# Decay exponential, rotated copies and six orderings in a two-layer hybrid decoder kernel

## The chip, the cores and the metric

The kernel runs on one core of a Trainium2 chip. The metric is the device time of one execution in microseconds. A comparison of two kernels takes timed runs of both on the same chip; beside them, one execution of each is profiled, and that one has a time of its own. All engine times in this document are from such a profile, counted from the start of its span.

The engines: TensorE (PE, with its weight loads as PEld), VectorE (DVE), ScalarE (ACT), GpSimd (POOL) and SyncE (SP), which issues the transfers. Each works through its own instructions strictly in the order they were laid down. They meet through semaphores.

## The reference, cut to what matters

Two layers over 512 tokens of width 1024, all in float32:

```python
def hybrid_layer(x, cos, sin, ...):
    xn = rmsnorm(x, norm1_g)
    proj = xn @ w_in          # split into SSD, MLA, GatedDeltaNet parts and three gate logits
    y_ssd = ssd_mixer(...)    # chunked scan; output normed in two groups of 512 channels
    y_mla = mla_mixer(mla_cq, mla_ckv, mla_kr, cos, sin, ...)
    y_gdn = gdn_mixer(...)
    mixed = g_ssd * (y_ssd @ w_ssd_out) + g_mla * (y_mla @ w_mla_out) + g_gdn * (y_gdn @ w_gdn_out)
    h = x + mixed @ w_out
    f = jnp.square(jax.nn.relu(rmsnorm(h, norm2_g) @ w_up)) @ w_down
    return h + f

def mla_mixer(cq, ckv, k_rope, cos, sin, q_norm_g, w_uq, kv_norm_g, w_ukv):
    q = (rmsnorm(cq, q_norm_g) @ w_uq)       # 8 heads of 128 plain + 64 rotated
    kv = (rmsnorm(ckv, kv_norm_g) @ w_ukv)   # 8 heads of 128 keys and 128 values
    k_pe = apply_rope(k_rope, cos, sin)      # one rotated key for all heads
    # scores = q_nope . k_nope + q_pe . k_pe, causal softmax, times v

a = -jnp.exp(a_log)                          # decay rates of SSD (and likewise of GatedDeltaNet)
```

A final RMS norm follows the second layer.

## The kernel before

**Precision.** A float32 product is made of three products of a faster kind: each operand is split into a high part (a rounding cast on ACT) and a low part (the difference, on DVE), and `mm3` (L196) issues high by high, high by low, low by high. So every weight tile and every activation needs one ACT and one DVE operation before PE can use it: `split_half` (L165; its rows are whi L170 and wlo L171) for weights, `split_act` (L268) and `split_gain` (L273, rows L274 and L275, with a gain per channel) for activations.

**Layout and staging.** Activations stand transposed, channels on partitions: `xh`, `xl` are eight tiles of 128 channels by 512 tokens. `norm_half` (L299) makes them for one half of the tokens: two token tiles are scaled by their inverse root mean square (xr, in the feed-forward f, L306), then turned by 16 transposes on PE (L311), four to a PSUM bank, each bank followed by two `split_gain`. The banks come from `sm_bank`, a rotating set of three; `y_bank` (tiles named yt) is a single bank beside them, `acc_bank` a set of four that products accumulate in. `norm_half` runs eight times: both halves of the first norm and of the second norm, in two layers.

**One layer.** The first products are those of the front: the key latent (256 wide, ck), the rotary key (64 wide, kr) and the step sizes, 352 columns in all (`front_weights`, L333, and `front`, L399). Then come the query latent (cq, L536), the transposes of the normed key latent (`latent`, L522), the rope tables in layer 0 (`rope_tables`, L119, sine and cosine on ACT) and attention in four pairs of heads (hp 0 to 3). `rope` (L545) swaps halves by four transfers on SP, multiplies by cosine (L551) and by sine (L552), adds. The rotated key kpe goes into kz0 and kz1, its rounded copy in one half of the partitions and zeros in the other, and into kps, the rounded copy below and the rest above. The rotated query of a pair of heads is cast to qph, and four transfers (L633) spread its halves over the tiles qps. The scores of a head and a query tile are five products: three of the plain part (L674 to L676), one of qps with kps (L677), one of qpl with kz (L678). The probabilities are turned on PE (L695) and multiplied with the values (L712 to L714).

The SSD and GatedDeltaNet branches follow, each SSD group normed by sums of squares that a product with ones makes (L832, one per chunk t of 128 tokens); between their steps PE runs output products of other branches (`out_proj`, L493). The output projection and the down projection use seven instead of eight block products (`seven`, L1204), for which DVE forms sums of weight blocks (`plus` in `seven_weights`, L1183, its row L1189). `up` (L1392) runs the up projection in four quarters qd of four blocks of 256 columns c each, through `dense_F` (L204).

`step_sizes` (L427) computes the decays, with aexp = exp(a_log) at L450, once per layer. ACT holds one set of function tables at a time: sine needs another set than exponential and tanh.

**What sets the order.** A planner puts each engine's instructions in order from what they depend on and from estimated costs. Code inside `tc.high_priority()` is placed as early as it can be. `behind(key, instruction)` (L153) makes the planner lay an instruction behind the one that `place(key, ...)` (L160) marks; `dense_F` and `dense_T` mark each weight tile of a tagged product by (tag, k, j). It is an order without a wait. So an edit at one place can move rows elsewhere.

## Time and profile before

| | |
|---|---|
| median of 3 runs | 2260.42 us (2259.19 to 2260.94) |
| the profiled execution's own time | 2263.41 us |
| its span, first to last instruction | 2261.6 us |
| mean granted clock of TensorE | 0.998 |
| PE, DVE, ACT, POOL busy | 2246.2, 1638.1, 1167.3, 65.7 us |
| read from HBM | 225.53 MB |

A row of a timeline gives the start, the duration, the engine, the line of the kernel, the operation, output and inputs, shapes, how many instructions it stands for, and in brackets the idle time of the engine before it and what ended it. [...] A row of windows gives the stretch, its length, then busy time and number of instructions of PE, PEld, DVE, ACT and POOL, the granted clock of PE, the share of the transfer engines and GB/s. A row of waits names who waited for whom: total, times, longest.

### The profile page before, as it was taken

Reading aid. Unit: us, or ns where it says so; the run is one execution under the profiler, and the core shown is the slowest. Engines: PE = TensorE matmul, PEld = TensorE weight load, DVE = VectorE, ACT = ScalarE, POOL = GpSimd, SP = SyncE. Lnnn points to the kernel's source line nnn. Section 1 sums busy time; section 2 is a strip of 40 time slices with the busy share of each in tenths; the row PEclk is TensorE's granted clock in tenths of the full one; section 3 lists DMA queues with packets and bytes.
Section 4 is the critical chain, followed back from the end, with each engine's and each line's share of the span. In section 5 each row is a group of like instructions: output and inputs, shape, how many; then the busy total and the mean of one; then the engine's idle time right before and its main releaser. Section 6 shows DMA issues by size and latency. Waiting matters only on the chain.

```text
span 2261.6 us, 32000 instructions
## 1 busy us (share of the span) xinstructions
PE 2246.2 (99%) x11758; PEld 1867.3 (83%) x11758; DVE 1638.1 (72%) x3259; ACT 1167.3 (52%) x2378; POOL 65.7 (3%) x84
## 2 busy tenths in 40 slices
PE   9999999999999999999999999999999999999998
PEld 8888787888888888888888888888888888888887
DVE  7777567876667778767877775678758668778668
ACT  6556644333443555554656566443335445645546
POOL 1000000000000000000010000000001000000000
PEclk9999999999999999999999999999999999999999
DMA  4333633452225143233133336335422251432231
GB/s 144 91 94 94 195 103 121 132 147 73 80 75 177 57 149 112 86 102 121 48 105 91 90 111 197 98 118 149 122 79 80 66 185 39 168 112 100 87 112 47
DMA packets 221310, 246.16 MB, mean 109 GB/s; under 512 B 34513, under 2 KB 172641, under 8 KB 221153
## 3 DMA queue, kind: packets, MB, share of 16 engines
q1 hardware_dynamic: 221008, 243.86, 35.3%
q8 instruction: 92, 1.51, 0.3%
q14 instruction: 66, 0.53, 0.1%
q10 hardware_dynamic: 144, 0.26, 0.0%
HBM read 225.53 MB, written 11.74 MB: 105 GB/s over the span
## 4 chain that ended last, share of the span: by engine, by line
PE 93%; DVE 3%; ACT 1%; DMA 1%; issue 1%; POOL 0%; SPq 0%; POOLq 0%; ACTq 0%; DVEq 0%
PE acc L198 24%; PE acc L202 23%; PE acc L201 23%; PE sm L202 3%; PE sm L198 3%; PE sm L201 3%; DVE wlo L171 1%; PE sm L695 1%; PE sm L1082 1%; PE sm L800 1%; PE yt L202 1%; PE yt L198 1%; PE yt L201 1%; PE sm L1108 1%; DVE ckl L737 1%
## 5 line engine op out<-in xcount | busy, mean ns | idle before, releaser
L171 DVE TENSOR_TENSOR wlo<-wraw,whi 128x512 fp32r<-128x512 f32 (+1 forms) x536 | 365.0, 686 | 328.8 <-ACT whi L170 321.7
L170 ACT CAST whi<-wraw 128x512 fp32r<-128x512 f32 (+1 forms) x536 | 329.5, 617 | 514.6 <-PE acc L201 347.1
L198 PE MATMUL acc<-xh,whi 128*128 128x512 f32 (+1 forms) x1344 | 525.5, 392 | 0.0
L202 PE MATMUL acc<-xh,wlo 128*128 128x512 f32 (+1 forms) x1344 | 520.5, 388 | 0.8 <-DVE wlo L171 0.8
L201 PE MATMUL acc<-xl,whi 128*128 128x512 f32 (+1 forms) x1344 | 519.1, 387 | 0.0
L202 PEld LDWEIGHTS acc<-xh,wlo 128*128 128x128 f32 x1344 | 252.6, 188 | 51.2 <-DVE wlo L171 1.8
L201 PEld LDWEIGHTS acc<-xl,whi 128*128 128x128 f32 x1344 | 252.9, 188 | 48.2 <-DVE xl L275 0.7
L198 PEld LDWEIGHTS acc<-xh,whi 128*128 128x128 f32 x1344 | 252.7, 188 | 48.2 <-ACT xh L274 0.4
L170 ACT CAST whi<-wr 128x512 fp32r<-128x512 f32 x168 | 104.4, 621 | 109.5 <-PE acc L201 47.2
L198 PE MATMUL acc<-yh,whi 128*128 128x512 f32 x384 | 152.4, 400 | 0.0
L201 PE MATMUL acc<-yl,whi 128*128 128x512 f32 x384 | 150.7, 392 | 0.0
L202 PE MATMUL acc<-yh,wlo 128*128 128x512 f32 x384 | 150.4, 392 | 0.0
L171 DVE TENSOR_TENSOR wlo<-wr,whi 128x512 fp32r<-128x512 f32 x168 | 113.1, 687 | 35.4 <-ACT whi L170 34.4
L737 DVE SCALAR_TENSOR_TENSOR ckl<-acc,pc,ckl 128x511 f32<-128x511 f32 (+2 forms) x168 | 120.8, 743 | 19.5 <-ACT ckl L733 10.3
L198 PEld LDWEIGHTS acc<-yh,whi 128*128 128x128 f32 x384 | 71.6, 188 | 16.1 <-ACT yh L274 2.2
L202 PEld LDWEIGHTS acc<-yh,wlo 128*128 128x128 f32 x384 | 72.2, 188 | 14.6
L201 PEld LDWEIGHTS acc<-yl,whi 128*128 128x128 f32 x384 | 72.2, 188 | 14.1
L198 PE MATMUL acc<-whi,xh 128*128 128x512 f32 (+1 forms) x208 | 80.0, 385 | 0.3 <-DVE ckl L737 0.3
L202 PE MATMUL acc<-whi,xl 128*128 128x512 f32 (+1 forms) x208 | 79.3, 381 | 0.0
L201 PE MATMUL acc<-wlo,xh 128*128 128x512 f32 (+1 forms) x208 | 79.3, 381 | 0.0
L488 ACT ACTIVATE eE<-eE,cum 128x128 f32<-128x128 f32 x192 | 63.7, 390 | 26.4 <-DMA eE<-d_c 23.5
L1228 DVE TENSOR_TENSOR h<-h,acc 128x512 f32<-128x512 f32 x120 | 77.0, 680 | 0.2
(475 smaller groups left out, 4471.1 us busy)
## 6 DMA issues: line engine op xcount, KB each, us to landing
wraw<-in_w_in_dram SPq DMA_DIRECT2D x144, 512.0 KB, 3.6
wraw<-in_w_up_dram SPq DMA_DIRECT2D x64, 512.0 KB, 3.6
wr<-in_w_down_dram SPq DMA_DIRECT2D x32, 1024.0 KB, 5.1
eE<-d_c SPq DMA_DIRECT2D x48, 256.0 KB, 4.5
wraw<-in_w_mla_out_dram SPq DMA_DIRECT2D x16, 512.0 KB, 3.3
eE<-d_e SPq DMA_DIRECT2D x32, 256.0 KB, 3.0
wraw<-in_w_ssd_out_dram SPq DMA_DIRECT2D x16, 512.0 KB, 3.4
wraw<-in_w_gdn_out_dram SPq DMA_DIRECT2D x16, 512.0 KB, 3.3
```

The costliest lines, as they stand in the source:

```text
L170: act.copy(hi, raw)
L171: dve.tensor_tensor(lo, raw, f32(hi), ALU.subtract)
L198: x = pe.matmul(o, ah, bh, start=start, stop=False, skip_group_check=more)
L201: pe.matmul(o, ah, bl, start=False, stop=False, skip_group_check=more)
L202: return pe.matmul(o, al, bh, start=False, stop=stop, skip_group_check=more)
L488: act.activation(o[:, i], o[:, i], AF.Relu, scale=-1.0, bias=cum[:, t, h0 + i : h0 + i + 1])
L695: pe.transpose(ps[:, n : n + P], pn[t][:, kb * P : (kb + 1) * P], ident)
L737: dve.scalar_tensor_tensor(acc[:, d:], ps[:, : S - d], taps_[3 - d], acc[:, d:], ALU.mult, ALU.add)
L800: x = pe.matmul(py[64 * i : 64 * i + 64, c * P : (c + 1) * P], xd[:, t, h * 64 : (h + 1) * 64], e2[h // 4][:, h % 4, :], start=True, stop= ...
L1082: x = pe.matmul(pw[:, h * P : (h + 1) * P], Y[:, h, :], r[:, h * P : (h + 1) * P], start=True, stop=True)
L1108: x = pe.matmul(po[:, h * P : (h + 1) * P], pt_[:, h, :], vn[:, h * P : (h + 1) * P], start=True, stop=True)
L1228: place((tag, n, t), dve.tensor_tensor(hs_, hs_, ps[t], op))
```

## The change

The edits, as they are numbered here:

1. The exponential of the decay rates (aexp) moves out of `step_sizes` to the start of the latent stage, with high priority, behind the cosine of the rope tables.
2. `split_half` can place its low part; layer 1's first two front weights have theirs behind the two scaled token tiles that `norm_half` makes at the end of layer 0 (key "scaled").
3. The last of `norm_half`'s four banks comes from `y_bank` instead of `sm_bank`, whose three banks the first three take.
4. The split of the key latent has high priority.
5. The rotated key is cast once (kph); three transfers on SP make kps's lower half and the two halves of kz from it, in place of three ACT casts.
6. The query's cast and its four transfers have high priority.
7. The SSD sum of squares of chunk t stands behind weight tile 2t+1 of an output product instead of 4t-5. For t = 2 that is 5 instead of 3; for t = 3 it is 7 both times.
8. For the first quarter of the down projection the weight sums stand behind tile (k = 1, j = 0) of the second block of the up product, which gets a tag for it.

```diff
@@ -141,7 +141,7 @@
         act.activation(sinT, r, AF.Sin, scale=inv_c[:, 1:2])
         dve.scalar_tensor_tensor(nn, r, -1.0, r, ALU.mult, ALU.max)
         dve.tensor_scalar(nn, nn, -1.0, float(np.float32(np.pi / 2)), ALU.mult, ALU.add)
-        act.activation(cosT, nn, AF.Sin)
+        place("rope", act.activation(cosT, nn, AF.Sin))
 
 
     seen_at, awaiting = {}, {}
@@ -162,13 +162,15 @@
         for i in awaiting.pop(key, ()):
             after_product(i, ins.ins)
 
-    def split_half(raw, hold=None, first=True):
+    def split_half(raw, hold=None, first=True, at=None):
 
         n = raw.shape[1]
         hi, lo = hold or (mk(wp, [P, n], F32R, "whi"), mk(wp, [P, n], F32R, "wlo"))
         with tc.high_priority() if first else nullcontext():
             act.copy(hi, raw)
-            dve.tensor_tensor(lo, raw, f32(hi), ALU.subtract)
+            x = dve.tensor_tensor(lo, raw, f32(hi), ALU.subtract)
+            if at:
+                behind(at, x)
         return hi, lo
 
     def weights_raw(w2d, c0, n, k0, kt):
@@ -296,16 +298,16 @@
         rsq(rs, rs, 1.0 / D, EPS)
         return rs
 
-    def norm_half(i, xs, ssq, gcol, pl, hs, ls, tag="xr", bufs=4, given=None, first=False):
+    def norm_half(i, xs, ssq, gcol, pl, hs, ls, tag="xr", bufs=4, given=None, first=False, at=None):
 
         xr = given or []
         for t in (2 * i, 2 * i + 1)[len(xr) :]:
             with tc.high_priority() if first else nullcontext():
                 rs = row_scale(ssq[t])
                 xr.append(mk(pl, [P, D], F32, tag, bufs))
-                dve.tensor_scalar(xr[-1], xs[t], rs, None, ALU.mult)
+                place(at, dve.tensor_scalar(xr[-1], xs[t], rs, None, ALU.mult))
         for k in range(0, KD, 2):
-            ps = sm_bank()
+            ps = sm_bank() if k < KD - 2 else y_bank()
             for j in range(4):
                 kk = k + j // 2
                 pe.transpose(ps[:, j * P : (j + 1) * P], xr[j % 2][:, kk * P : (kk + 1) * P], ident)
@@ -338,7 +340,7 @@
             raw = raws[q] if given else front_raw(ly, q)
             for i in range(2):
                 hold = [mk(lp, [P, NF], F32R, "mix", 8) for _ in range(2)] if q < 2 else None
-                res.append(split_half(raw[:, i * NF : (i + 1) * NF], hold, not given or q == 1))
+                res.append(split_half(raw[:, i * NF : (i + 1) * NF], hold, not given or q == 1, ("scaled", ly) if ly and q < 2 else None))
         return res
 
     h_pool = ExitStack()
@@ -419,6 +421,9 @@
         ml = mp.enter_context(tc.tile_pool(name="ml", bufs=1, reuse_waits="tile"))
         if ly == 0:
             rope_tables(ml)
+        aexp = mk(sp, [P, 24], F32, "aexp", 2)
+        with tc.high_priority():
+            behind("rope", act.activation(aexp, prow[:, 24:48], AF.Exp))
 
         cum = mk(sp, [P, T, 24], F32, "cum")
         d_c, d_p = (mk(dr, [T, 24 * P], F32, n, 2) for n in ("d_c", "d_p"))
@@ -446,8 +451,6 @@
             dve.tensor_scalar(v, v, 0.0, None, ALU.max)
             spl = w24("spl")
             dve.scalar_tensor_tensor(spl, e1, 2.0, v, ALU.mult, ALU.add)
-            aexp = mk(sp, [P, 24], F32, "aexp")
-            act.activation(aexp, prow[:, 24:48], AF.Exp)
             g24 = mk(sp, [P, T, 24], F32, "g24")
             dve.scalar_tensor_tensor(g24, spl, -1.0, bc_mid(aexp, T), ALU.mult, ALU.mult)
             ps = sm_bank()
@@ -527,7 +530,8 @@
                 ps = sm_bank()
                 for t in range(T):
                     behind(((ly, "q", 0), 1, 2), pe.transpose(ps[:, t * P : (t + 1) * P], tok[t][:, k * P : (k + 1) * P], ident))
-                split_gain(hs[k], ls[k], ps, col(gi + k))
+                with tc.high_priority():
+                    split_gain(hs[k], ls[k], ps, col(gi + k))
             return hs, ls
 
         cqh, cql = hilo_tags(ml, "cq", 4)
@@ -563,12 +567,14 @@
         kpe = rope(kd)
         kz = [mk(ml, [P, S], F32R, f"kz{j}") for j in range(2)]
         kps = mk(ml, [P, S], F32R, "kps")
+        kph = mk(lp, [P, S], F32R, "mix", 8)
+        act.copy(kph, kpe)
+        dve.tensor_tensor(kps[64:], kpe[64:], f32(kph[64:]), ALU.subtract)
+        sync.dma_start(f32(kps[:64]), f32(kph[:64]))
         for j in range(2):
             half, other = (slice(64 * i, 64 * i + 64) for i in (j, 1 - j))
             pool.memset(f32(kz[j][other]), 0.0)
-            act.copy(kz[j][half], kpe[half])
-        act.copy(kps[:64], kpe[:64])
-        dve.tensor_tensor(kps[64:], kpe[64:], f32(kz[1][64:]), ALU.subtract)
+            sync.dma_start(f32(kz[j][half]), f32(kph[half]))
 
         query_latent(1)
         ckh, ckl = latent(lp, ck_tok, 256, g_kv, "ck")
@@ -625,12 +631,13 @@
             qr = rope(qp)
 
             qph, qpl = (mk(ml, [P, S], F32R, nm) for nm in ("qph", "qpl"))
-            act.copy(qph, qr)
+            qps = [mk(ml, [P, S], F32R, f"qps{j}") for j in range(2)]
+            with tc.high_priority():
+                act.copy(qph, qr)
+                for j in range(2):
+                    for i in range(2):
+                        sync.dma_start(f32(qps[j][64 * i : 64 * i + 64]), f32(qph[64 * j : 64 * j + 64]))
             dve.tensor_tensor(qpl, qr, f32(qph), ALU.subtract)
-            qps = [mk(ml, [P, S], F32R, f"qps{j}") for j in range(2)]
-            for j in range(2):
-                for i in range(2):
-                    sync.dma_start(f32(qps[j][64 * i : 64 * i + 64]), f32(qph[64 * j : 64 * j + 64]))
             wkv = list(weights(a["mla_w_ukv"][ly], hp * 512, 512, 256))
             with tc.high_priority(30):
                 ks = head_tiles(dense_F(wkv, [slice(0, P), slice(256, 256 + P)], 256, ckh, ckl), "k")
@@ -831,7 +838,7 @@
                 dve.tensor_tensor(sq[:, 0], sq[:, 0], sq[:, 1], ALU.add)
                 x = pe.matmul(pss[:, t : t + 1], sq[:, 0], ones[:, 0:1], start=True, stop=True)
                 if t > 1:
-                    behind(((ly, 1, 2 * g, "y"), 4 * t - 5, 0), x)
+                    behind(((ly, 1, 2 * g, "y"), 2 * t + 1, 0), x)
             rs = mk(sp, [P, T], F32, "srs")
             rsq(rs, pss[:, :T], 1.0 / 512, EPS)
             ps = sm_bank()
@@ -1180,13 +1187,15 @@
         hpl = h_pool.enter_context(tc.tile_pool(name="hp", bufs=1, reuse_waits="tile"))
         last = ly == depth - 1
         ssq = [mk(sp, [P, 2], F32, "nss", 4) for _ in range(T)]
-        def seven_weights(pl, w2d, r0):
+        def seven_weights(pl, w2d, r0, sums_at=None):
 
             b = {}
 
             def plus(o, x, y):
                 for q in (slice(0, 1024), slice(1024, 2048)):
-                    dve.tensor_tensor(o[:, q], x[:, q], y[:, q], ALU.add)
+                    z = dve.tensor_tensor(o[:, q], x[:, q], y[:, q], ALU.add)
+                    if sums_at:
+                        behind(sums_at, z)
 
             def after(c):
                 i, j = ((0, 0), (0, 1), (1, 1), (1, 0))[c]
@@ -1420,7 +1429,7 @@
                     banks = None
                     if qd > 0 and c < 2:
                         banks = [sm_bank(), sm_bank() if c else y_bank()]
-                    for j, ps in enumerate(dense_F(weights(a["w_up"][ly], qd * 1024 + c * 256, 256, D), tiles(256), D, xh, xl, mid, banks)):
+                    for j, ps in enumerate(dense_F(weights(a["w_up"][ly], qd * 1024 + c * 256, 256, D), tiles(256), D, xh, xl, mid, banks, tag=None if qd else (ly, "u", c))):
                         act.activation(f[:, j * S : (j + 1) * S], ps, AF.Relu)
                     act.activation(f, f, AF.Square)
                     t0, t1 = (fk(f)[:, :, hf] for hf in HALVES)
@@ -1440,7 +1449,7 @@
 
             def down_weights(qd):
 
-                return seven_weights(fp, a["w_down"][ly], qd * D)
+                return seven_weights(fp, a["w_down"][ly], qd * D, None if qd else ((ly, "u", 1), 1, 0))
 
             def ends(qd):
 
@@ -1459,7 +1468,7 @@
                     for t in range(2):
                         fin(t)
                     if not last:
-                        norm_half(0, hts, h_ssq, lambda k: params[0][:, 124 + k : 125 + k], fp, *nx, "f", 4, first=True)
+                        norm_half(0, hts, h_ssq, lambda k: params[0][:, 124 + k : 125 + k], fp, *nx, "f", 4, first=True, at=("scaled", ly + 1))
 
                 return dict(sq=h_ssq, before_last=before_last, fin=fin, prep=prep, early=not last, tag=(ly, "d"),
                             settled=(lambda r, j: settle(r, j, gb[0])) if last else None)
```

Where rows move. First PE at the key latent in layer 0. The names: acc_797 (acc_801 in the change) holds the first head's keys, its products read ckh and ckl; yt and acc_691 (acc_695) hold queries. Before:

```order
L202 MATMUL acc_692<-cqh_91_454,wlo_729 128x512
L198 MATMUL yt_693<-cqh_91_454,whi_728 128x512
L201 MATMUL yt_693<-cql_95_458,whi_728 128x512
L202 MATMUL yt_693<-cqh_91_454,wlo_729 128x512
L198 MATMUL acc_797<-ckh_138_660,whi_789 128x512
L201 MATMUL acc_797<-ckl_140_662,whi_789 128x512
L198 MATMUL acc_691<-cqh_92_455,whi_743 128x512
```

The change:

```order
L204 MATMUL acc_696<-cqh_92_456,wlo_733 128x512
L200 MATMUL acc_801<-ckh_140_664,whi_793 128x512
L200 MATMUL yt_697<-cqh_92_456,whi_732 128x512
L203 MATMUL acc_801<-ckl_142_666,whi_793 128x512
L203 MATMUL yt_697<-cql_96_460,whi_732 128x512
L204 MATMUL acc_801<-ckh_140_664,wlo_794 128x512
L204 MATMUL yt_697<-cqh_92_456,wlo_733 128x512
```

The first product of ckh comes three rows earlier, between two query products, and the one of ckl two rows later than that.

ACT in the same stage (pn are squares of the query latent, mix the copy of the rotary key that `rope` starts from, cqh the query latent). Before:

```order
L274 ACTIVATE cqh_90_453<-acc_477,pc_122 128x512
L541 ACTIVATE pn_115_548<-acc_476 128x512
L562 COPY mix_560<-sm_555 128x512
L541 ACTIVATE pn_116_552<-acc_477 128x512
L141 ACT_TABLE_LOAD
L141 ACTIVATE sinT_85<-qh_424,inv_c_77 128x512
L144 ACTIVATE cosT_80<-qh_427 128x512
```

The change:

```order
L276 ACTIVATE cqh_91_455<-acc_479,pc_122 128x512
L141 ACT_TABLE_LOAD
L141 ACTIVATE sinT_85<-qh_424,inv_c_77 128x512
L545 ACTIVATE pn_116_550<-acc_478 128x512
L144 ACTIVATE cosT_80<-qh_427 128x512
L426 ACT_TABLE_LOAD
L426 ACTIVATE aexp_448<-prow_124 128x24
L426 ACTIVATE aexp_11193<-prow_8044 128x24
L545 ACTIVATE pn_117_554<-acc_479 128x512
L566 COPY mix_562<-sm_557 128x512
```

Two exponentials (of layer 0 and layer 1) and the second table load follow the cosine, and the copy of the rotary key stands behind them, not ahead of the sine's load. Before, the exponential of layer 1 with its table load stood right ahead of the splits of the key latent.

PE at the start, in the first half norm. Before:

```order
L311 MATMUL sm_188<-ct_75,xr_137 128x128
L311 MATMUL sm_188<-ct_75,xr_138 128x128
L198 MATMUL acc_252<-mix_210,xh_25_154 128x352
L201 MATMUL acc_252<-mix_211,xh_25_154 128x352
L198 MATMUL acc_253<-mix_210,xh_25_154 128x352
L202 MATMUL acc_252<-mix_210,xl_33_162 128x352
```

The change:

```order
L313 MATMUL sm_188<-ct_75,xr_137 128x128
L313 MATMUL sm_188<-ct_75,xr_138 128x128
L313 MATMUL yt_197<-ct_75,xr_137 128x128
L313 MATMUL yt_197<-ct_75,xr_138 128x128
L313 MATMUL yt_197<-ct_75,xr_137 128x128
L313 MATMUL yt_197<-ct_75,xr_138 128x128
L200 MATMUL acc_252<-mix_210,xh_25_154 128x352
```

All 16 transposes now stand together, the last four into yt; before, they came ten rows after the first product.

## The prediction

> **What bounds the kernel now.** I read the page first, then the waits of PE, then the timeline at each wait.
>
> ```profile
> PE 2246.2 (99%) x11758; PEld 1867.3 (83%) x11758; DVE 1638.1 (72%) x3259; ACT 1167.3 (52%) x2378; POOL 65.7 (3%) x84
> PE 93%; DVE 3%; ACT 1%; DMA 1%; issue 1%; POOL 0%; SPq 0%; POOLq 0%; ACTq 0%; DVEq 0%
> PE acc L198 <- ACT ckh L274: 1.0, 1, 1.0
> PE sm L311 <- DVE xr L379: 0.9, 1, 0.9
> PE sm L677 <- DMA qps<-qph: 0.8, 2, 0.6
> PE acc L202 <- DVE wlo L171: 0.8, 1, 0.8
> PE yt L832 <- ACT eE L488: 0.7, 2, 0.4
> PE acc L201 <- DVE ckl L275: 0.5, 1, 0.5
> ```
>
> TensorE sets the end: busy 99%, 93% of the chain. The change leaves its products as they are, so it can only win PE's rests. The waits (total, times, longest) add up to some 8 us, and most of them stand at lines that the diff touches. A rest also costs the refill of PE, so below I count from start to start: products of 128x512 start every 0.23 us, those of 128x256 every 0.12, transposes every 0.11, and what exceeds that is lost.
>
> **Part 1: the key latent (decay exponential, key copies, latent splits).**
>
> ```profile
> 59.05 0.39 PE L202 MATMUL yt<-cqh,wlo 128*128 128x512 f32 x1
> 60.46 0.50 PE L198 MATMUL acc<-ckh,whi 128*128 128x512 f32 x1 [1.01 <-ACT ckh L274]
> 61.46 0.50 PE L201 MATMUL acc<-ckl,whi 128*128 128x512 f32 x1 [0.50 <-DVE ckl L275]
> 44.21 0.58 ACT L562 COPY mix<-sm 128x512 f32<-128x512 f32 x1
> 54.01 0.62 ACT L570 CAST kps<-mix 64x512 fp32r<-64x512 f32 x1
> 56.79 1.28 ACT L450 ACT_TABLE_LOAD   x1
> 58.08 0.22 ACT L450 ACTIVATE aexp<-prow 128x24 f32<-128x24 f32 x1
> 59.72 1.27 ACT L274 ACTIVATE ckh<-sm,pc 128x512 fp32r<-128x512 f32 x2
> 60.66 1.40 DVE L275 SCALAR_TENSOR_TENSOR ckl<-sm,pc,ckh 128x512 fp32r<-128x512 f32 x2
> 51.25 0.68 DVE L552 TENSOR_TENSOR mix<-mix,sinT 128x512 f32<-128x512 f32 x1
> mix<-mix SPq DMA_DIRECT2D x4, 64.0 KB, 2.5
> ```
>
> From 59.05 the next start should be 59.28, it is 60.46; the one after should be 60.69, it is 61.46: 1.18 + 0.77 = 1.95 us. ACT came late with ckh because the table load and aexp (1.5 us) and three half casts (about 1.9) stood ahead of it. All that leaves. But the table load does not vanish: it moves behind the cosine, and so ahead of the copy of kd, which feeds the rope's swap transfers. I place the copy (L562) by its place in ACT's new order: it ended at 44.8 and now ends at about 48.8 (ACT: sine, cosine at about 46.1, load 1.28, two exponentials, one square, copy). SP then issues four swaps of 0.6 us each, the last lands 2.5 us after its issue, at about 53.8, where L552 now runs at 51.25. DVE stands behind it: that product with the sine (0.6 from start to start), eight more operations of 0.34 to 0.66, together 4.6, and the first ckl itself (0.7) give a first ckl at about 59.7. PE's new order asks for it at 58.9. So I keep a rest of 0.8 and book a gain of **1.15** (bounds 0, if the chain is a microsecond later than I place it, and 1.95). The three key transfers replace casts; each SP issue takes 0.6, a landing 2.5, and kps and kz are first read by the first scores, more than 40 products (9 us) behind the latent: nothing. If that cover were gone, the scores would wait the 2.5. The new rest, if any, waits for ckl behind L552, no longer for ckh.
>
> **Part 2: the clock behind that rest.**
>
> ```profile
> 61.00:62.00 1.00, 0.54 (x2) 0.49 (x3) 1.00 (x3) 0.61 (x2) 0.00 (x0) 1.00 0.02 6
> 63.00:64.00 1.00, 1.00 (x3) 0.73 (x3) 0.00 (x0) 0.16 (x1) 0.00 (x0) 0.50 0.60 223
> 65.00:66.00 1.00, 1.00 (x4) 0.80 (x3) 0.16 (x1) 0.00 (x0) 0.00 (x0) 0.50 0.00 0
> 66.00:67.00 1.00, 1.00 (x5) 0.81 (x5) 0.05 (x1) 0.68 (x2) 0.00 (x0) 0.97 0.00 0
> ```
>
> The number before the last two is the granted clock: it halves for some 3.4 us right after the two rests, and eight products start 0.43 us apart, not 0.23: 8 x 0.2 = 1.6 us, nowhere else before the kernel's end. One rest of 0.8 should not do that, since the single rests of 0.6 to 1.1 elsewhere did not: gain **1.6** (bounds 0 and 1.6).
>
> [...]
>
> **Part 3: the last bank of each half norm in another PSUM bank.**
>
> ```profile
> 799.08 0.63 PE L311 MATMUL sm<-ct,f 128*128 128x128 f32 x4 [0.16 <-DVE xl L275]
> 808.73 1.47 PE L311 MATMUL sm<-ct,f 128*128 128x128 f32 x12
> 811.77 0.63 PE L311 MATMUL sm<-ct,f 128*128 128x128 f32 x4
> 817.25 0.40 PE L198 MATMUL acc<-xh,whi 128*128 128x512 f32 x1
> 11.31 0.43 PE L198 MATMUL acc<-mix,xh 128*128 128x352 f32 x1 [0.33 <-ACT xh L274]
> 13.69 0.63 PE L311 MATMUL sm<-ct,xr 128*128 128x128 f32 x4
> ```
>
> Twelve transposes fill three banks, the last four wait for the first bank to be split. Second half of the second norm: 808.7 to 817.2 are 8.5 us for 16 transposes and 48 products of 256, which alone are 16 x 0.11 + 48 x 0.12 = 7.5. With all 16 first, the splits start as before but PE asks for them 0.44 later, and is spared a change between kinds of work: of the 1.0 I take 0.8, twice (two layers). First half: 799.08 should be 798.76; with the change of kind 0.4, twice. Start, layer 0's second and layer 1's second half, where narrower products chase the splits in the same way: 0.5 + 0.4 + 0.4, by the rest of 0.33 at 11.31 and the transposes at 13.69 in the midst of the products; layer boundary 0.1. Together **3.8** (bounds 1, if the splits only become late elsewhere, and 5).
>
> **Part 4: four single rests.**
>
> ```profile
> 1127.66 0.52 DVE L171 TENSOR_TENSOR mix<-wraw,mix 128x352 fp32r<-128x352 f32 x1
> 1129.50 1.42 PE L311 MATMUL sm<-ct,f 128*128 128x128 f32 x11 [0.36 <-DVE f L306]
> 161.55 2.41 SPq L633 DMA_DIRECT2D qps<-qph  x4
> 166.58 0.36 PE L677 MATMUL sm<-kps,qps 128*128 128x256 f32 x1 [0.55 <-DMA qps<-qph]
> 1286.86 0.36 PE L677 MATMUL sm<-kps,qps 128*128 128x256 f32 x1 [0.25 <-DMA qps<-qph]
> 249.16 0.97 ACT L488 ACTIVATE eE<-eE,cum 128x128 f32<-128x128 f32 x3
> 250.25 0.35 PE L832 MATMUL yt<-ct,wk 128*128 128x1 f32 x2 [0.45 <-ACT eE L488]
> 816.80 1.23 DVE L1189 TENSOR_TENSOR wp<-wr,wr 128x1024 f32<-128x1024 f32 x1 [2.34 <-DMA wr<-in_w_down_dram]
> 818.68 0.50 PE L202 MATMUL acc<-xh,wlo 128*128 128x512 f32 x1 [0.80 <-DVE wlo L171]
> ```
>
> Layer boundary: one weight split of 0.44 (next row's start less its own) between the two scalings leaves; of 0.53 lost at 1129.50 I take **0.45** (bounds 0, 0.53).
> Rotated query: PE lost 0.71 at 166.58 and 0.41 at 1286.86, both at the fourth head pair. On ACT and SP the four transfers keep their neighbours in the new order; what changes is PE, where three products of 128x512 (0.68) now stand ahead of the first product that reads qps. That covers layer 0; layer 1 likewise: **1.0** (bounds 0, 1.1).
> SSD sums: of the four sums over chunk 2, behind ACT's exponentials, the worst lost 0.6 and all four 1.3. They now stand two weight tiles, twelve products or 2.7 us, later, and their next reader waits for chunk 3's sum anyway: **1.2** (bounds 0, 1.3).
> Weight sums: one addition, itself waiting 2.34 for its transfer, held the split that PE needed, 0.97 lost. Behind the second tile of that product it is followed by splits for the next block of columns, and a block is 48 products, 10.9 us: the four sums of 1.2 fit: **0.9** (bounds 0, 0.97).
>
> **The other side of the bill.** The planner has also rearranged attention: value products now stand before the score products of the next head, and fewer products are left behind the scores for the softmax.
>
> ```profile
> 148.11 0.39 PE L678 MATMUL sm<-kz,qpl 128*128 128x512 f32 x1
> 151.21 0.71 PE L695 MATMUL sm<-ct,pn 128*128 128x128 f32 x5
> ```
>
> From the last score to its transposes the old order had 3.1 us. In the new one I count 3.6 to 3.8 us of work between them at this head, and I take **+1.2** in all for sixteen heads, an estimate (bounds 0 and 3).
>
> Sum: 1.15 + 1.6 + 3.8 + 0.45 + 1.0 + 1.2 + 0.9 = 10.1 won, 1.2 lost, net 8.9. The profiled execution took 2263.41 (span 2261.6 and 1.8 around it) and would take 2254.5; it lies 3.0 above the median, so the runs' median of 2260.42 becomes **2251.5**. From no change a measurement here can tell 0.2%, 4.5 us: faster is below 2255.9.
>
> **Rivals.**
> *The chain at the latent eats the start.* If DVE's range reduction and swaps do not move with PE, what the start wins (0.9) is waited away at ckl, that rest stays near 1.95, the clock still halves: 0.9 + 1.15 + 1.6 = 3.65 less, 2255.2. For it: 60.66 is DVE work with no idle ahead; against: three casts and a table load left ACT.
> *It does not do what it says.* The priority moves neither cast nor transfer of the query, and the SSD sums meet other exponentials: 2.2 less, 2253.7. For it: the unchanged neighbours on ACT and SP.
> *The other side: softmax without cover.* Place: the transposes behind the last score of each of sixteen heads. If ACT and DVE deliver the probabilities 1.5 us later than now, because weight splits come between, the cover of 0.5 to 0.7 that I counted is used up and each head rests about 1.0: 16 us against the 10.1 won, 2266.3. It turns the change into a loss from 0.63 us a head (10.1 / 16), and passes the measurement's 4.5 from 0.9. Against it: DVE is busy 72%, and where I counted, the cover has grown.
>
> **How the numbers follow.** Forecast 0.62, latent chain 0.20, not what it says 0.11, softmax 0.07. The forecast alone spans 2248.5 to 2255.5 by its bounds. Down, all gains whole and no new wait give 2247.5; up, the first two rivals reach 2255 and with other unknown costs 2259.5: range 2247.5 to 2259.5. Faster 0.73 (0.58 + 0.07 + 0.08), same 0.21 (0.04 + 0.13 + 0.03 + 0.01), slower 0.06, from the last rival.
>
> **What would show it.** Right: no granted clock below 1 between 60 and 70 us; transposes in runs of 16; no wait of PE at the query copies, at the SSD sums over chunk 2, at the scaled rows of the boundary or behind the weight sums; table load between 46 and 50 us. Wrong: L552's successor waiting for a swap beyond 54 us with PE waiting for ckl over 1 us, half clock there, or new waits of PE at the softmax transposes that add to more than 3 us.

## The result, and the profile after

The changed kernel takes 2252.08 us (median of 5 runs, 2251.47 to 2252.57), the kernel before on the same chip 2260.43 us: a ratio of 0.9963 with a 95% interval of 0.995 to 0.9976, or 8.35 us less. The forecast was 2251.5, with 2247.5 to 2259.5 as its range. The profiled execution took 2251.97 us with a span of 2250.2, and its granted clock stays at 1.00 up to 2245 us, where the kernel runs out.

The busy line and all waits of PE that the profile of the changed kernel still lists:

```profile
PE 2240.5 (100%) x11758; PEld 1866.6 (83%) x11758; DVE 1639.1 (73%) x3259; ACT 1162.0 (52%) x2374; POOL 67.2 (3%) x84
PE yt L354 <- POOL cosT L109: 1.0, 1, 1.0
PE acc L200 <- DVE ckl L744: 0.4, 2, 0.2
PE acc L200 <- ACT xh L276: 0.3, 1, 0.3
PE sm L313 <- DVE xr L381: 0.2, 1, 0.2
```

Of the six waits that the prediction quoted five are gone from the list (ckh, qps, wlo, eE, ckl of the latent), and xr, at the start, is down from 0.9 to 0.2. Apart from the start only the two short ones at ckl L744, a line of another branch, are left. Line numbers have grown by 2 to 9: the products are now L200, L203 and L204, the norm's transposes L313, split_gain L276 and L277, the first product with qps L684.

The key latent in the timelines of PE, ACT, DVE and SP, the last row from the windows:

```profile
58.07 0.39 PE L200 MATMUL acc<-ckh,whi 128*128 128x512 f32 x1
58.30 0.39 PE L200 MATMUL yt<-cqh,whi 128*128 128x512 f32 x1
58.81 0.50 PE L203 MATMUL acc<-ckl,whi 128*128 128x512 f32 x1
44.88 0.63 ACT L144 ACTIVATE cosT<-qh 128x512 f32<-128x512 f32 x1 [0.80 <-DVE qh L143]
45.52 1.28 ACT L426 ACT_TABLE_LOAD   x1
47.53 0.58 ACT L566 COPY mix<-sm 128x512 f32<-128x512 f32 x1
56.46 1.27 ACT L276 ACTIVATE ckh<-sm,pc 128x512 fp32r<-128x512 f32 x2
52.17 0.69 DVE L556 TENSOR_TENSOR mix<-mix,sinT 128x512 f32<-128x512 f32 x1
58.01 1.40 DVE L277 SCALAR_TENSOR_TENSOR ckl<-sm,pc,ckh 128x512 fp32r<-128x512 f32 x2
50.74 0.53 SPq L179 DMA_DIRECT2D wraw<-in_mla_w_ukv_dram  x1
63.00:64.00 1.00, 1.00 (x7) 0.82 (x5) 1.00 (x3) 0.82 (x3) 0.00 (x0) 1.00 0.00 0
```

The product with ckh starts without a rest. Products of 128x512 last 0.39 us in these rows and start 0.23 apart (58.07 to 58.30); from 58.30 the next start would be 58.53, and ckl lets it come at 58.81: 0.28 of the 1.95 us is left, counted from start to start. The cosine ends near 45.5 (the prediction had 46.1), the table load follows at once, a little ahead of the 46 to 50 us that the prediction named, and the copy of kd ends at 48.1 (48.8). The first of the two ckl is done near 58.7, 1.0 before the 59.7 of the prediction. The clock stays at 1.00 where it had halved.

The other places, in the timelines of PE and, in the last two rows, of DVE:

```profile
164.87 0.39 PE L684 MATMUL sm<-kps,qps 128*128 128x512 f32 x1
248.50 0.28 PE L839 MATMUL yt<-ct,wk 128*128 128x1 f32 x2
802.61 1.47 PE L313 MATMUL sm<-ct,f 128*128 128x128 f32 x12
803.92 0.60 PE L313 MATMUL yt<-ct,f 128*128 128x128 f32 x4
1120.94 1.62 PE L313 MATMUL sm<-ct,f 128*128 128x128 f32 x12
809.84 2.05 DVE L171 TENSOR_TENSOR wlo<-wraw,whi 128x512 fp32r<-128x512 f32 x3 [0.32 <-ACT whi L170]
811.80 1.22 DVE L1196 TENSOR_TENSOR wp<-wr,wr 128x1024 f32<-128x1024 f32 x1
```

Transposes run in twelves and fours, sixteen on end; neither qps, nor the SSD sum, nor the transposes at the layer boundary (1120.94) have a wait in brackets; on DVE the splits that PE needs stand ahead of the weight addition.

### The profile page after: what moved, and what is told of

It reads as the page before. It is cut to its first block, busy times and chain, and to the rows that moved or that the text cites. A ratio compares the mean times of both kernels' runs of the same rounds, so it can differ in the third digit from the quotient of the medians.

```text
span 2250.2 us, 32003 instructions
## 1 busy us (share of the span) xinstructions
PE 2240.5 (100%) x11758; PEld 1866.6 (83%) x11758; DVE 1639.1 (73%) x3259; ACT 1162.0 (52%) x2374; POOL 67.2 (3%) x84
## 4 chain that ended last, share of the span: by engine, by line
PE 96%; DVE 2%; DMA 0%; issue 0%; POOL 0%; ACT 0%; SPq 0%; POOLq 0%; ACTq 0%; DVEq 0%
PE acc L200 25%; PE acc L204 24%; PE acc L203 24%; PE sm L204 3%; PE sm L203 3%; PE sm L200 3%; PE sm L702 1%; PE sm L807 1%; PE sm L1089 1%; PE sm L818 1%; PE sm L1115 1%; PE yt L204 1%; PE yt L203 1%; PE yt L200 1%; DVE ckl L744 1%; PE sm L1103 1%
## 5 line engine op out<-in xcount | busy, mean ns | idle before, releaser
L200 PE MATMUL acc<-xh,whi 128*128 128x512 f32 (+1 forms) x1344 | 525.4, 391 | 0.0
L204 PE MATMUL acc<-xh,wlo 128*128 128x512 f32 (+1 forms) x1344 | 520.1, 387 | 0.0
L203 PE MATMUL acc<-xl,whi 128*128 128x512 f32 (+1 forms) x1344 | 518.8, 386 | 0.0
L204 PEld LDWEIGHTS acc<-xh,wlo 128*128 128x128 f32 x1344 | 252.6, 188 | 49.7 <-DVE wlo L171 0.4
L200 PEld LDWEIGHTS acc<-xh,whi 128*128 128x128 f32 x1344 | 252.8, 188 | 48.4 <-ACT xh L276 0.5
L203 PEld LDWEIGHTS acc<-xl,whi 128*128 128x128 f32 x1344 | 252.9, 188 | 47.7
L200 PE MATMUL acc<-yh,whi 128*128 128x512 f32 x384 | 152.7, 401 | 0.0
L203 PE MATMUL acc<-yl,whi 128*128 128x512 f32 x384 | 150.6, 392 | 0.0
L204 PE MATMUL acc<-yh,wlo 128*128 128x512 f32 x384 | 150.0, 391 | 0.0
L744 DVE SCALAR_TENSOR_TENSOR ckl<-acc,pc,ckl 128x511 f32<-128x511 f32 (+2 forms) x168 | 120.9, 744 | 18.3 <-ACT ckl L740 10.3
L200 PEld LDWEIGHTS acc<-yh,whi 128*128 128x128 f32 x384 | 71.5, 188 | 16.2 <-ACT yh L276 2.3
L204 PEld LDWEIGHTS acc<-yh,wlo 128*128 128x128 f32 x384 | 72.1, 188 | 14.8
L203 PEld LDWEIGHTS acc<-yl,whi 128*128 128x128 f32 x384 | 72.2, 188 | 13.8
L200 PE MATMUL acc<-whi,xh 128*128 128x512 f32 (+1 forms) x208 | 79.8, 384 | 0.4 <-DVE ckl L744 0.4
L203 PE MATMUL acc<-wlo,xh 128*128 128x512 f32 (+1 forms) x208 | 79.4, 382 | 0.0
L204 PE MATMUL acc<-whi,xl 128*128 128x512 f32 (+1 forms) x208 | 79.2, 381 | 0.0
```

The costliest lines, as they stand in the source:

```text
L200: x = pe.matmul(o, ah, bh, start=start, stop=False, skip_group_check=more)
L203: pe.matmul(o, ah, bl, start=False, stop=False, skip_group_check=more)
L204: return pe.matmul(o, al, bh, start=False, stop=stop, skip_group_check=more)
L744: dve.scalar_tensor_tensor(acc[:, d:], ps[:, : S - d], taps_[3 - d], acc[:, d:], ALU.mult, ALU.add)
```

## The experiments

The eight edits keep their numbers. Twelve kernels ran on three chips (the first four on one, the next four on a second, the last four on a third), and the kernel before ran beside each group: 2260.55, 2261.0 and 2260.51 us. The column of gains is against the group's own. The twelfth, e12, adds work to the changed kernel and stands at the end.

| kernel | edits in it | median, us | runs | gain, us |
|---|---|---|---|---|
| the change | all | 2252.08 | 5 | 8.35 |
| e1 | none | 2260.67 | 10 | -0.1 |
| e2 | all but 1 | 2251.07 | 4 | 9.5 |
| e3 | all but 5 | 2252.01 | 5 | 8.5 |
| e4 | all but 1, 4, 5 | 2251.45 | 4 | 9.1 |
| e5 | all but 3 | 2257.85 | 10 | 3.15 |
| e6 | 3 alone | 2255.88 | 10 | 5.1 |
| e7 | all but 6 | 2253.20 | 5 | 7.8 |
| e8 | all but 2, 7, 8 | 2254.21 | 6 | 6.8 |
| e9 | all | 2251.98 | 5 | 8.5 |
| e10 | 2, 3, 6, 7 | 2251.66 | 5 | 8.85 |
| e11 | all but 3, 5 | 2255.97 | 10 | 4.5 |

**e1: the kernel before, profiled a second time.** No edit.

> The kernel before, unchanged, profiled a second time. Question: why the profiled execution of before took 2263.4 when its median is 2260.4, and whether the half clock behind the key latent belongs to every execution. Theory (the clock's window runs freely against the kernel): the rests at the first ckh and ckl products are again 1.1 to 1.2 and 0.7 to 0.8 us, but the half clock need not come; without it the span is 2258 to 2260. Rival (the two rests always trigger it): half clock for 3.4 us again, span 2261 to 2262.

Measured: 2260.67 us (2259.07 to 2261.38), ratio 1.0 (0.9991 to 1.0009). The profiled execution took 2261.14, against 2263.41 the first time. Its timelines of PE, ACT and DVE, and one of its windows:

```profile
60.01 0.49 PE L198 MATMUL acc<-ckh,whi 128*128 128x512 f32 x1 [0.72 <-ACT ckh L274]
61.01 0.50 PE L201 MATMUL acc<-ckl,whi 128*128 128x512 f32 x1 [0.51 <-DVE ckl L275]
816.51 0.50 PE L202 MATMUL acc<-xh,wlo 128*128 128x512 f32 x1 [0.99 <-DVE wlo L171]
48.27 0.62 ACT L144 ACTIVATE cosT<-qh 128x512 f32<-128x512 f32 x1
56.34 1.28 ACT L450 ACT_TABLE_LOAD   x1
59.27 1.27 ACT L274 ACTIVATE ckh<-sm,pc 128x512 fp32r<-128x512 f32 x2
50.78 0.69 DVE L552 TENSOR_TENSOR mix<-mix,sinT 128x512 f32<-128x512 f32 x1
63.00:64.00 1.00, 1.00 (x6) 0.84 (x5) 0.44 (x1) 0.52 (x1) 0.00 (x0) 1.00 0.11 38
```

The two rests are there again (0.88 and 0.78 from start to start, 1.66 together), but no half clock follows. So the 1.6 us of Part 2 belonged to the first profiled execution, not to every one; none of the 61 executions of the kernel before that ran beside the experiments or as e1 took more than 2262.25, and the mean granted clock of each was 0.999 or 1.0, not the 0.998 of the first profile. The record of the clock moves in steps of 3.413 us, counted from its first rise (the half clock lasted one step), and that rise comes at 4.63 us in the first profile and at 6.36 in this one: as far as these steps are the theory's window, it did run freely against the kernel. Against this second profile the changed kernel gains 9.3 us in the trace, not 11.6.

**e2, e3, e4: the three edits at the latent, undone one by one and together.** Each is cut from the changed kernel:

```diff
 e2, edit 1:
-        with tc.high_priority():
-            behind("rope", act.activation(aexp, prow[:, 24:48], AF.Exp))
+            act.activation(aexp, prow[:, 24:48], AF.Exp)      # in step_sizes, as before
 e3, edit 5:
-        act.copy(kph, kpe)
-        sync.dma_start(f32(kps[:64]), f32(kph[:64]))
-            sync.dma_start(f32(kz[j][half]), f32(kph[half]))
+            act.copy(kz[j][half], kpe[half])
+        act.copy(kps[:64], kpe[:64])
 e4, edits 1, 4 and 5: both of these, and
-                with tc.high_priority():
-                    split_gain(hs[k], ls[k], ps, col(gi + k))
+                split_gain(hs[k], ls[k], ps, col(gi + k))
```

> The changed kernel with the decay exponential back in the step sizes, so that its table load stands between weight casts again. Theory (the load or the key casts, each alone, fit into ACT's idle time; only both together make ckh late): rest at the first ckl product at most 0.5 us, no half clock, time 2252 to 2253. Rival (the load alone made it late): a rest of 1.2 or more at ckh and a time of 2254 to 2256.

> The changed kernel with the three half casts of the rotated key on ACT again, no key transfers. Theory (either alone is covered): ckh comes about a microsecond later than in the change, rest at the ckh and ckl products at most 0.6 us together, no half clock, 2252 to 2253. Rival (the casts made it late): 1.2 or more, 2254 to 2256.

> The changed kernel with all three edits at the key latent undone: exponential, key copies, priority of the latent splits. Theory: ckh is late again, rests of 1.3 to 2.0 us together at the first ckh and ckl products, and the half clock where the window falls so: 2253.5 to 2255.7. Rival (the gain there came from the other edits, by PE's order at that place): rests below 0.6 us, 2252 to 2253.

Measured: 2251.07, 2252.01 and 2251.45 us, ratios 0.9957 (0.9943 to 0.9972), 0.9962 (0.9948 to 0.9976) and 0.996 (0.9945 to 0.9975). None loses anything: the rests at the latent are under 0.13 in e2, 0.28 and 0.33 in e3, 0.29 in e4. The time of e2 even lies below both of its theories, and its four runs (2250.47 to 2251.38) lie below all ten of the changed kernel (2251.47 to 2252.78, e9 included). They did not run side by side with it, so that edit 1 costs up to 1 us is a hint and not shown; the rows point the same way, since without the early load the copy of kd starts at 45.88 (in e4, which lacks edit 1 too), with it at 47.53. With all three undone, e4's timelines of ACT, DVE and PE read:

```profile
44.87 0.63 ACT L144 ACTIVATE cosT<-qh 128x512 f32<-128x512 f32 x1 [0.99 <-DVE qh L143]
47.48 1.28 ACT L452 ACT_TABLE_LOAD   x1
49.53 0.22 ACT L452 ACTIVATE aexp<-prow 128x24 f32<-128x24 f32 x1 [0.76 <-DVE g L454]
52.07 1.25 ACT L571 CAST kz<-mix 64x512 fp32r<-64x512 f32 x2 [0.41 <-DVE mix L555]
56.97 1.26 ACT L276 ACTIVATE ckh<-sm,pc 128x512 fp32r<-128x512 f32 x2
50.62 0.69 DVE L554 TENSOR_TENSOR mix<-mix,sinT 128x512 f32<-128x512 f32 x1
58.56 0.50 PE L203 MATMUL acc<-ckl,whi 128*128 128x512 f32 x1
```

The theory of Part 1 fell here, as far as it names the edits. The half casts are back on ACT, and ckh is still 2.3 us earlier than in e1. The rope does not bring it: its product with the sine starts at 50.62, in e1 at 50.78. What differs is the work that ACT has ahead of ckh. In e1 the table load and the exponential stand there (56.34 to 57.8, 1.4 us), with one more split of the query latent. In e4 the cosine is 3.4 us earlier, and the load and the exponential follow it at 47.48 and 49.53, in a stretch where ACT has to wait anyway (0.76). So the load does leave the way to ckh, as Part 1 held, but without the edits that were to move it. Another edit had to have moved it, and the cosine with it.

**e5, e6: the last bank (edit 3) undone, and alone.**

```diff
 e5: cut from the changed kernel (e6: every other edit cut, this line kept)
-            ps = sm_bank() if k < KD - 2 else y_bank()
+            ps = sm_bank()
```

> The changed kernel with the last bank of each half norm back in the ring of three (edit 3 undone). Undoing the three edits at the key latent had left the gain there whole. The new theory is that the gain at the latent comes from this edit: it changes ScalarE's order at the start, so that the sine and the cosine of the rotation tables stand ahead of the copy of the rope input instead of behind it, and the whole chain to ckh runs some 3 us earlier. New theory: the rests at ckh and ckl come back in part although the exponential and the key copies stay where the change put them (0.5 to 1.6 us), the second norms lose 2.2, the start 0.3, the halves of layer 1 some 0.3; together 3.5 to 4.4, so 2255.6 to 2256.5 us. Rival (the query's edit 6 or the shared order makes the latent early): no rest at the latent beyond 0.3, and only Part 3's own 2.8 is lost, 2254.9. The prediction's own sum for this part, 3.8, would give 2255.9 with the latent as in the changed kernel.

> The kernel before with only edit 3, the last bank of each half norm in another PSUM bank. New theory: the latent's rests fall from 1.66 us to under 0.4 without any edit at the latent, and with the start (0.3), both second norms (2.2) and layer 1's halves (0.3) the gain is 4.0 to 4.5, so 2256.0 to 2256.5 us against 2260.5. Rival: the latent keeps its two rests of 0.88 and 0.78, and the gain is 2.8, 2257.7.

Measured: e5 2257.85 us (2256.87 to 2259.78), ratio 0.9987 (0.9978 to 0.9996); e6 2255.88 (2254.95 to 2256.65), ratio 0.9978 (0.9968 to 0.9987). This one line is worth 5.1 us alone, more than half of the whole change, and without it the other seven are worth 3.15. The rows of e6, from the timelines of PE and DVE:

```profile
58.85 0.50 PE L203 MATMUL acc<-ckl,whi 128*128 128x512 f32 x1
810.95 0.69 DVE L171 TENSOR_TENSOR wlo<-wraw,whi 128x512 fp32r<-128x512 f32 x1 [1.13 <-ACT whi L170]
812.43 1.23 DVE L1191 TENSOR_TENSOR wp<-wr,wr 128x1024 f32<-128x1024 f32 x1 [0.79 <-DMA wr<-in_w_down_dram]
246.70 0.35 PE L834 MATMUL yt<-ct,wk 128*128 128x1 f32 x2 [1.03 <-ACT eE L490]
```

At the latent only 0.3 is lost (58.85 behind 58.32), as the new theory said; the gain is above the 4.0 to 4.5 that it gave. The second and third row are what no theory had: in e6 one weight split stands ahead of the late addition on DVE, and PE's 0.99 of e1's 816.51 does not occur, though edit 8 is not in this kernel. The last row is the other side: alone, edit 3 makes the first SSD sum 1.19 late, and by its list of waits PE waits 1.0 in all for the query's transfers, which edits 7 and 6 then mend.

e5 was worse than its theory, which let the gain be 4.0 us at the least. Its timelines of PE, SP and ACT say why:

```profile
60.64 0.50 PE L200 MATMUL acc<-ckh,whi 128*128 128x512 f32 x1 [1.89 <-ACT ckh L276]
53.06 0.51 SPq L573 DMA_DIRECT2D kps<-mix  x1
53.62 1.24 SPq L577 DMA_DIRECT2D kz<-mix  x2
54.95 0.54 SPq L179 DMA_DIRECT2D wraw<-in_mla_w_ukv_dram  x1
58.87 1.14 ACT L170 CAST whi<-wraw 128x512 fp32r<-128x512 f32 x2 [1.48 <-DMA wraw<-in_mla_w_ukv_dram]
```

PE rests 2.05 at ckh, more than in the kernel before. In this order, with the cosine late again (48.05), the three key transfers of edit 5, which wait for the rope, stand ahead of the transfer of the key and value weights on SP. Those are asked for at 54.95 instead of 50.74, their cast waits 1.48 for them, and ckh stands behind that cast.

The ten runs of e5 fall into two groups. Four had a mean granted clock of 0.998, as the first profile of the kernel before had, and took 2258.94 us on average. The other six, the profiled one among them, had 0.999 and took 2257.50. The 1.4 us between them is near the 1.6 of Part 2, so half clock probably came again in those four; none of them was profiled, so where it came is not shown. By the six alone (median 2257.41) the gain of e5 is 3.6.

**e11: without edits 3 and 5,** to test that reading (the cuts of e5 and e3 together).

> The changed kernel without edit 3 and without edit 5: the bank in the ring again and the key's copies made by ScalarE's casts instead of transfers. Without edit 3 alone PE rested 2.05 us at ckh, and there SyncE issued the three key transfers, which wait for the rope, ahead of the transfer of the key and value weights that ckh's engine had to cast first. New theory: that queue is the cause; with the casts back the weights are asked for at about 50.5 us instead of 54.95, the rest at ckh falls under 0.6, and the time to 2256.0 to 2256.6. Rival: without edit 3 the late cosine alone makes ckh late (as in the kernel before: 0.88 and 0.78); rests of 1.5 or more together, 2257.5 to 2258.

Measured: 2255.97 us (2255.39 to 2256.51), ratio 0.998 (0.9971 to 0.9989). From its timelines of SP and PE:

```profile
52.27 0.38 SPq L179 DMA_DIRECT2D wraw<-in_mla_w_ukv_dram  x1
58.24 0.51 PE L200 MATMUL acc<-ckh,whi 128*128 128x512 f32 x1 [0.46 <-ACT ckh L276]
59.24 0.50 PE L203 MATMUL acc<-ckl,whi 128*128 128x512 f32 x1 [0.27 <-DVE ckl L277]
```

Taking edit 5 out makes this kernel faster by 1.4 us of gain (4.5 against 3.15), or by about 0.9 against the six runs of e5 with the clock of 0.999. The rests fall from 2.12 together (2.05 and 0.07) to 1.06 (0.63 and 0.43), and no row of ACT waits for these weights: the queue on SP was the cause. The 0.63 is a hair over the bound of the theory, and the weights are asked for at 52.27, not the 50.5 that it named. That the rests are 1.06 together and not e1's 1.66 may be what edits 1 and 4 are worth where the cosine is late; they were not tried alone there.

**e7: the query without priority (edit 6 undone).**

```diff
-            with tc.high_priority():
-                act.copy(qph, qr)
-                ...
+            act.copy(qph, qr)
             dve.tensor_tensor(qpl, qr, f32(qph), ALU.subtract)
+            # the four transfers here, as before
```

> The changed kernel with the rotated query's copy and its four transfers without priority (edit 6 undone); by the program's order this alone puts attention back into its order of before, value products behind the next head's scores. Theory 1 (the prediction): the two waits for the query's transfers return, 1.1 us, and the extra rests at the softmax transposes go, up to 1.2 by the prediction: 2251.9 to 2252.3, no difference in time. Theory 2 (the new order costs nothing, as the aligned traces suggest: no wait of PE there but some 0.14 at a few heads): 1.1 lost and 0.5 back at most, 2252.6 to 2253.2. Rival: the early latent hangs on this edit, and its rests of 1.66 come back too, 2254.5.

Measured: 2253.20 us (2252.8 to 2253.53), ratio 0.9965 (0.9952 to 0.9978). The latent keeps its early ckh (56.27 on ACT). The query waits return, in the timeline of PE:

```profile
162.25 0.39 PE L683 MATMUL sm<-kps,qps 128*128 128x256 f32 x1
1279.15 0.36 PE L683 MATMUL sm<-kps,qps 128*128 128x256 f32 x1 [0.93 <-DMA qps<-qph]
```

0.27 and 1.09 from start to start, 1.36 together. Against them nothing comes back for the old order: in neither kernel does the list of waits have PE waiting at the softmax transposes, and from 20 us to the end the trace of e7 loses 2.0 us against that of the changed kernel, more than the two waits. So the rearranged attention has no price, which is theory 2. The gain against the group's own kernel before is 0.55 to 0.7 smaller than with the edit, by the medians as they are it is 1.1 to 1.2; such differences are near what runs can tell, and the rows carry the verdict.

**e8: the boundary's split, the SSD sums and the weight sums back (edits 2, 7 and 8 undone).**

```diff
-                    behind(((ly, 1, 2 * g, "y"), 2 * t + 1, 0), x)
+                    behind(((ly, 1, 2 * g, "y"), 4 * t - 5, 0), x)
-                return seven_weights(fp, a["w_down"][ly], qd * D, None if qd else ((ly, "u", 1), 1, 0))
+                return seven_weights(fp, a["w_down"][ly], qd * D, None)
-... not given or q == 1, ("scaled", ly) if ly and q < 2 else None))
+... not given or q == 1))
```

> The changed kernel with the SSD sums, the sums of the down weights and the splits at the layer boundary back where they were (edits 2, 7, 8 undone). By the prediction's terms 1.2 + 0.9 + 0.45 = 2.55 come back: 2254.6 us. By the aligned traces of before and after they are worth more, SSD 2.7 (two sums in each layer gain 1.0 and 0.4), weight sums 1.3, boundary 0.4, together 4.4: 2256.5 us. The waits that should be seen again: yt waiting for ACT eE (0.5 or so) at the sums over chunk 2, acc waiting for DVE wlo (0.8) behind the weight sums, sm waiting for DVE xr or f at the boundary.

Measured: 2254.21 us (2253.47 to 2255.17), ratio 0.997 (0.9958 to 0.9982): 1.6 us less gain than the whole change, 1.9 by the traces, in which e8's start happens to be 0.66 shorter than the changed kernel's. Two of the three waits are back, in the timeline of PE:

```profile
244.81 0.35 PE L839 MATMUL yt<-ct,wk 128*128 128x1 f32 x2 [0.39 <-ACT eE L491]
1121.98 0.77 PE L313 MATMUL sm<-ct,f 128*128 128x128 f32 x5 [0.37 <-DVE f L308]
```

Of the 4.4 us that the aligned traces had promised, 2.8 come back stage by stage: 2.35 at the SSD groups and 0.4 at the boundary. The third wait, 0.8 behind the weight sums, is not seen: as in e6, with edit 3 in place a split stands ahead of the addition. In e5, which has edit 8 and not edit 3, it is absent too. So either edit removes it, and beside edit 3 edit 8 is worth nothing.

**e9, e10: the changed kernel again, and edits 2, 3, 6 and 7 alone,** side by side. e10 is the changed kernel with the cuts of e4 and the second cut of e8.

> The changed kernel itself once more, beside the next three on one chip: the yardstick for differences under 1 us between kernels. All theories: 2252.1 us, within 0.7 of it, and no clock below 1 anywhere; the start's first rests (1.0 us in the first profile) may come out 0.5 smaller or larger.

> The kernel before with only four of the eight edits: the last bank (3), the boundary's split (2), the rotated query (6) and the SSD sums (7); the exponential, the latent's priority, the key's transfers (1, 4, 5) and the weight sums (8) left as before. New theory: beside edit 3 the other four are idle, because the order that edit 3 brings already puts sine and cosine early and one weight split ahead of the late addition; time as the changed kernel's within 0.7 us, no rest over 0.4 at ckh or ckl, no wait for wlo near 815 us. The prediction's terms would give 1.15 (latent) + 0.9 (weight sums) = 2.05 more, 2254.1, and 1.6 on top in an execution whose clock halves.

Measured: e9 2251.98 us (2251.66 to 2252.78), ratio 0.9963 (0.9949 to 0.9976); e10 2251.66 (2250.89 to 2252.24), ratio 0.996 (0.9948 to 0.9973). The four edits do all of it; their runs overlap with those of the whole change, so e10 is not shown to beat it, only to be as fast with half of the edits. The rest at ckl is 0.30 in e10 and 0.46 in e9, and e10's list of waits has none for wlo.

**e12: rests of graded length for the clock.** In the first profile of the kernel before, the clock had halved behind rests of 1.18 and 0.77 us, in e1 not behind 0.88 and 0.78. The question was what other lengths do.

```diff
+                        behind((rest, 3, 1), pe.transpose(first[:, :P], ident, ident))
+                        act.copy(scratch, first[:, :P])
+                        for _ in range(2 * (2 * (qd - 1) + c - 2) + 1):
+                            act.copy(scratch, scratch)
+                        place(("rested",) + rest[1:], pe.transpose(second[:, :P], scratch, ident))
```

> The changed kernel with twelve rests of PE added, six in each layer's feed-forward: a transpose, a chain of 2, 4, 6, 8, 10 and 12 small copies on ScalarE, and a transpose that waits for the chain and that the next products wait for; extra work whose result is not used. By copies of 0.2 to 0.3 us the rests should be about 0.7 to 3.5 us, the whole some 20 to 28 us longer. [...]

Measured: 2268.81 us, one run, 16.7 more than the changed kernel. Eight of the twelve chains were covered by the products between; four rests came out, two of 1.07 us and two of 2.78. The first of the two long ones in PE's timeline, and the window behind it:

```profile
1095.91 0.33 PE L1442 MATMUL sm<-ct,scr 128*128 128x128 f32 x1 [2.61 <-ACT scr L1441]
1096.00:1097.00 1.00, 1.00 (x5) 0.83 (x6) 0.31 (x2) 0.62 (x1) 0.00 (x0) 1.00 0.00 0
```

The clock behind both is 1.00, and it is below 1 in no microsecond window of that kernel before its end. So one rest of 2.78 us did not halve it where it stood here, nor did 2.05 in the profiled execution of e5 or 1.66 in e1. In the first profile of the kernel before it halved behind 1.95 (1.18 and 0.77, like the others from start to start).

The traces do not settle why. In the first profile of the kernel before, 17 steps of 3.413 us lie between the first rise of the clock at 4.63 and the half clock at 62.66, which lasts one step, and 642 between its end and the fall at 2257.43; in the profile of the changed kernel 656 lie between the rise at 6.84 and the fall at 2245.98. In the first profile of the kernel before, the step ahead of the half clock, 59.24 to 62.66, holds 1.5 us of idle PE. Counted the same way from the first rise at 6.36, a step of e1 holds 1.2 (57.56 to 60.97), and one of e12, counted back from the fall at 2262.44, holds 1.8 (1091.68 to 1095.09); neither was followed by half clock. So the idle time in one step does not decide it either, and the cause stays open.

## Why the prediction was right or wrong, point by point

The table sets the terms of the sum against the two traces. Each number is the gain over one stage: the k-th product of a name in one trace is set against the k-th of that name in the other, and the median difference of their starts at the end of a stage, less that at its beginning, is what the stage gained.

| term | predicted | first profile of before, to the change | second profile (e1), to the change |
|---|---|---|---|
| Part 1, the latent | 1.15 | 2.0 | 1.6 |
| Part 2, the clock | 1.6 | 1.3 | -0.2 |
| Part 3: start | 0.5 | 0.5 | 0.4 |
| Part 3: both second norms | 2.4 | 2.0 | 2.2 |
| Part 3: other halves and boundary | 0.9 | 0.3 | 0.3 |
| Part 4: boundary split | 0.45 | 0.5 | 0.5 |
| Part 4: query, less the rearranged attention | 1.0 - 1.2 | 1.4 | 1.2 |
| Part 4: SSD sums | 1.2 | 2.3 | 2.1 |
| Part 4: weight sums | 0.9 | 1.3 | 1.2 |
| sum | 8.9 | 11.6 | 9.3 |

**The time was right, and partly by errors that cancel.** Against the second profile two steps were too high, the clock by 1.8 and the small halves of Part 3 by 0.6; four were too low, attention by 1.4, the SSD sums by 0.9, the latent and the weight sums together by 0.8. (The medians differ by 8.35, the two profiled executions by 9.2: that of e1 lies 0.5 above its median.) The range, which held, does not come out of the terms either: all upper bounds together and no price give 2248.0, all lower bounds with the full price of 3 give 2262.4, not 2247.5 and 2259.5.

**The start** is no evidence either way. Two profiles of the changed kernel, the first and e9, show it in their timelines of PE. L354 is 22 products with zeros, 44 rows, ahead of the first scaled rows:

```profile
0.98 7.95 PE L354 MATMUL yt<-cosT 128*128 128x128 f32 x44 [0.98 <-POOL cosT L109]
9.23 1.42 PE L313 MATMUL sm<-ct,xr 128*128 128x128 f32 x11 [0.18 <-DVE xr L381]
0.98 6.71 PE L354 MATMUL yt<-cosT 128*128 128x128 f32 x44 [0.98 <-POOL cosT L109]
8.95 1.42 PE L313 MATMUL sm<-ct,xr 128*128 128x128 f32 x11 [0.90 <-DVE xr L381]
```

The 44 start every 0.21 us at first, later every 0.11; the faster pace comes at 6.7 us in the first profile and at 4.1 in e9. In e9 they end earlier, so the rest behind them is longer (1.1 against 0.35 from start to start), and yet the scaled rows come earlier. From 10 to 60 us e9 is 0.6 to 0.8 ahead of the first profile, with equal times at the end. So the 0.4 to 0.5 that the table has for the start lies within what one kernel does by itself.

**Part 1** had the right place and credited the wrong edits. Of "all that leaves", the table load and the exponential do count: they make 1.4 of the 2.3 us by which ckh comes earlier in e4 than in e1. The half casts do not: e3 and e4 have them back beside edit 3 and lose nothing. But edit 3 alone takes the load out of the way (e6, where the rest falls to 0.3), and the load stays away when the three edits at the latent are undone beside it (e4). The step that failed is that the sum took edit 3 for a matter of transposes alone; it did not ask which edit had put sine, cosine and with them the load so early.

The size was 0.45 too low. The new order was read rightly: the load stands ahead of the copy of kd, and ckl is then what PE waits for. The times were counted down too late: the copy ended at 48.1 instead of 48.8, the product with the sine ran at 52.17 instead of 53.8, the chain on DVE behind it took 6.5 instead of 5.9, so the errors partly cancel, and the first ckl was done near 58.7 instead of 59.7.

The sentence "The three key transfers replace casts ... nothing" looked only at who reads kps and kz. What it left out is who stands behind them on SP: where the cosine is late (e5) the key and value weights do, and the three cost PE about 1.1 us of rest (2.12 against 1.06 in e11).

**Part 2** booked for the median what one execution had shown. The second profile and the 61 executions did not slow down (mean granted clock 0.999 or 1.0 in each), and without the term the sum is 2253.1. Why the first profile did is not shown: by the steps counted at e12, one step of e1 held nearly all of both rests. The term should have been left out of the median, since it rested on one execution whose time lay 3.0 above it.

**Part 3.** The second norms are right (2.4 against 2.0 to 2.2, and e5 loses 1.1 at each). The halves that narrower products chase were sized by a single rest at the start and brought 0.3, not 0.9.

**Part 4.** The boundary split is right. The rotated query is right in its mechanism: the first product with qps, at 164.87, follows its predecessor by 0.23, and e7 brings 1.36 back. The weight sums are right in size, and edit 8 is enough for them (e5), but so is edit 3 alone (e6), so that beside it edit 8 adds nothing (e8). The SSD sums were under-sized: the term counted the sums over chunk 2 (1.3 in all) and held that the next reader waits for chunk 3's sum anyway. e8 against the change loses 1.25 in layer 0 and 1.1 in layer 1. Of that, 0.55 is the first sum's start at 244.81, and 0.25 stands at the product with the scale srs at 254.48, that next reader; the rest lies in the other groups.

**The other side of the bill**, +1.2 for rearranged attention, did not come. The price had no row behind it.

**The rivals.** "The latent chain eats the start" did not happen: 0.28 of rest, no half clock. "It does not do what it says" neither. "Softmax without cover" is excluded: no wait of PE at the softmax transposes is in the list of waits.

## What to carry to other kernels

An edit in a planned kernel acts in two ways, by what it does and by the order in which everything else is laid, and the second can count as much: one line about a PSUM bank was worth 5.1 us alone, where all eight edits bring 8.4. It brought a cosine 3.1 us forward (45.16 in e6, 48.27 in e1), and two rests that are not at its transposes went with that order, 1.35 of 1.66 at the latent and 0.99 at a weight split. So credit for a vanished wait goes to an edit only when the wait stays away with this edit alone, and comes back without it; here the three edits aimed at the latent failed both halves of that test (e5 has all three without edit 3, and PE rests 2.1; e4 lacks them, and it rests 0.3), and the weight sums had two sufficient edits. The casts that became transfers were not free where what stood behind them in the queue could not wait: in e5 the key and value weights were asked for at 54.95 us instead of 50.74, and PE rested 2.12, against 1.06 with the casts (e11).
